# Operations on freshly loaded tiles are issued behind their engine's earlier work, and attention takes slightly less dense work beside it

## The chip, the cores and the metric

The kernel runs on one core of one Trainium2 chip. The metric is device time in microseconds (us): the median of three runs before the change is 2832.04 us, the runs lie between 2825.74 and 2834.8 us. TensorE (PE in the profile) multiplies matrices, VectorE (DVE) and ScalarE (ACT) work on tiles in SBUF and PSUM, GpSimd (POOL) does a few fills, and SyncE (SP) issues nearly all DMAs. Each engine works through its own list of instructions in the order in which the built program has them. An instruction that waits for a DMA or for another engine holds up everything behind it on its own list.

## The reference, cut to what matters

One encoder layer runs over two sequences, of 1024 and 2048 tokens (samples 0 and 1 below), with 16 learned tokens ahead of each.

```python
xn = _rmsnorm(h, g_pre)
proj = xn @ w_in + b_in
na_q, na_k, na_v, na_z, ml_qk, ml_v, ml_z, ml_o, ml_g, mg = jnp.split(proj, SPLIT_IDX, axis=-1)
ya = _neighbourhood_attention(na_q, na_k, na_v, na_rpb)
ya = (ya * jax.nn.silu(na_z)) @ w_a
yb = (_mlstm_branch(ml_qk, ml_v, ml_g, ml_o, ml_conv_w, ml_head_g) * jax.nn.silu(ml_z)) @ w_b
ga, gb = jnp.split(jax.nn.sigmoid(mg), 2, axis=-1)
y = (ga * ya + gb * yb) @ w_out
return h + _rmsnorm(y, g_post)
```

Attention has 8 heads of width 64 with a window of 8 rows and 16 columns; the mLSTM has 4 heads of width 128 and runs in chunks, forward and backward. All is float32: each product is made of three products of a high and a low part (hi times hi, hi times lo, lo times hi).

## The kernel before

Two programs are woven into one order of TensorE instructions. **Dense** work is a list of groups (`PLAN`): input projections of 1024 tokens each, then six **merges** (`final`, L1464 to L1589), one for each block of 512 tokens. A merge multiplies the branch outputs by `w_a` and `w_b` in 8 steps of two products each (half `br` 1, the mLSTM, then `br` 0, attention), gates and adds them on DVE (L1502 to L1506), and then runs an output stage of 16 turns through `w_out` (L1536 to L1538). ACT squares each result (L1566) and DVE scales it by `g_post` into the tile `yo` (L1567). The residual rows `xres` are added behind that (`final_out`, L1617), beside the next merge's products. **Sparse** work is, in this order, the mLSTM of sample 0 (`ml`), attention of sample 0 (`na`), the mLSTM of sample 1 and attention of sample 1. Each sparse step yields a number of microseconds, and `run` (L1669) draws dense work of that planned length behind it: `A_NA` for a step of attention (four steps for one unit, 128 units in sample 1), `A_A` for a step of the mLSTM's second part.

TensorE's order is the order in which the code is written and drawn (`manual_schedule` for PE alone). The order on DVE, ACT, POOL and SP is made by a scheduler when the program is built: it goes by its own estimate of when each instruction can start, that of a DMA's landing included. So an operation on a tile that a DMA fills can be placed well ahead of where the code has it.

What the change touches:

- `na_prep` (L804): for each attention head, `qr`, `kr` and `vr` are loaded and split into high and low parts (L835, L840, L845 on ACT, L838, L842, L847 on DVE).
- `conv` (L1060): the first tap of the mLSTM's convolution on the loaded tile `raw` (L1066, ACT).
- `ml_outputs` (L1215): `kv` splits the loaded `kf` (L1267), `decay` adds the triangular mask to the loaded `um` (L1274, DVE; then two exponentials on ACT, L1276), `state` splits the loaded `va` into `vh` (L1284, ACT) and `vl` (L1285, DVE). A block of 256 tokens takes six steps: scores of block b+1 (TensorE into the bank `sc`, which DVE reads at L1308), then `back(b, 0)`, whose products read `vh` and `vl`, and so on; `finish` and, for every second block, the head's norm (`ml_norm`, L1398 to L1422) follow.
- `yload` (L1425): a merge's eight tiles `yl` (four of attention, from `ya`; four of the mLSTM, from `yb`) are loaded at least seven calls ahead, copied to `yh` (L1455, ACT) and reduced to the low part (L1440, DVE). It runs beside the output stage of the merge before.
- `final` L1520: the one scaling of the loaded `g_post` row (`gain`), and `final_out` L1617.

Of the kernel before, what the change touches and what calls it, by code (L numbers as in the profile page):

```python
# [2 lines left out]

# [1 line left out]

# [4 lines left out]
F32 = mybir.dt.float32  # L10
F32R = mybir.dt.float32r
I32 = mybir.dt.int32
AF = mybir.ActivationFunctionType
ALU = mybir.AluOpType
# [100 lines left out]

NBW = 4
C512, C256 = 0.235, 0.12
A_NA, A_D, A_A, A_G = 1.1, 1.63, 1.82, 1.3


class K:
# [15 lines left out]
    def rsqrt8(self, pool, v, shape):  # L137

        nc = self.nc
        y = pool.tile(shape, F32, name="nwy", bufs=2)  # L140
        t = pool.tile(shape, F32, name="nwt", bufs=2)
        nc.vector.tensor_scalar(y.bitcast(I32), v.bitcast(I32), 1, None, op0=ALU.logical_shift_right)
        nc.vector.tensor_scalar(y.bitcast(I32), y.bitcast(I32), -1.0, MAGIC, op0=ALU.mult, op1=ALU.add)
        for n in range(3):
            nc.vector.scalar_tensor_tensor(t, y, 0.25 ** n, y, op0=ALU.mult, op1=ALU.mult)
            nc.vector.tensor_tensor(t, t, v, op=ALU.mult)
            nc.vector.scalar_tensor_tensor(y, t, 3.0, y, op0=ALU.subtract, op1=ALU.mult)
        return y

    def psum(self, tag, shape):  # L150
        return self.pp.tile(shape, F32, name=tag, tag=tag, bufs=BANKS[tag])
# [652 lines left out]
    def na_prep(self, np_, s, rows, heads, j):  # L804

        nc, i = self.nc, self.i
        rt, pr, hh = heads[j]
        typ, lo, nr = rows[rt]
        ns, h0 = nr + 1, hh * 64
        ms, rs = ((nr, 0), (nr, 0), (0, 1))[typ]  # L810
        qr = np_.tile([P, 512], F32, name="qr", bufs=1)
        stk = np_.tile([P, 4, P], F32R, name="stk", bufs=2)
        qb = self.qB[hh]
        nc.sync.dma_start(qr[0:64], self.NQ[s][pr][h0:h0 + 64, rt * 512:(rt + 1) * 512])
        sv = stk.rearrange("p b t -> p (b t)")
        kr = np_.tile([P, 16, 64], F32, name="kr", bufs=1)
        kd = np_.tile([P, 16, 64], F32R, name="kd", bufs=2)
        kx = self.kx[hh]
        self.twice(kr[:, rs:rs + nr, :].rearrange("p a b -> p (a b)"), self.NK[s][pr], h0, lo * 64)
        self.twice(kr[:, ms, :], self.NKM[pr], h0, 0)  # L820
        ks = 8 * ns
        if hh == 0:
            self.vr = np_.tile([P, 8, P], F32, name="vr", bufs=1)
            f0 = pr * P
            nc.sync.dma_start(self.vr[ms * 8:ms * 8 + 8], self.NVM[:, f0:f0 + P].rearrange("(b c) f -> c b f", c=8))
            nc.sync.dma_start(self.vr[rs * 8:(rs + nr) * 8],
                              self.NV[s][:, lo * 8:(lo + nr) * 8, f0:f0 + P].rearrange("b q f -> q b f"))
            self.zt = np_.tile([P, 512], F32, name="zt", bufs=2)
            nc.sync.dma_start(self.zt, self.NZ[s][pr][:, rt * 512:(rt + 1) * 512])
            self.yg = np_.tile([P, 512], F32, name="yg", bufs=2)  # L830
        vr, zt, yg = self.vr, self.zt, self.yg
        if j < 2 or rows[heads[j - 2][0]][0] != typ:
            nc.gpsimd.dma_start(kx[64:128, :ns, :].rearrange("p a b -> p (a b)"), i["masks"][typ, :, :ns * 64])
        yield
        nc.scalar.activation(sv[0:64], qr[0:64], AF.Copy)  # L835
        yield
        nc.scalar.activation(qb[0:64], stk[0:64].bitcast(F32), AF.Copy)
        nc.vector.tensor_tensor(sv[64:128], qr[0:64], sv[0:64].bitcast(F32), op=ALU.subtract)  # L838
        yield
        nc.scalar.activation(kd[:, :ns, :], kr[:, :ns, :], AF.Copy)  # L840
        yield
        nc.vector.tensor_tensor(kx[0:64, :ns, :], kr[0:64, :ns, :], kd[0:64, :ns, :].bitcast(F32), op=ALU.subtract)  # L842
        vt = np_.tile([P, 8, 2, 64], F32R, name="vt", bufs=2)
        vv = vr[:ks, :, h0:h0 + 64]
        nc.scalar.activation(vt[:ks, :, 0], vv, AF.Copy)  # L845
        yield
        nc.vector.tensor_tensor(vt[:ks, :, 1], vv, vt[:ks, :, 0].bitcast(F32), op=ALU.subtract)  # L847
        self.head = stk, qb, kd, vt, yg, zt
        yield
# [210 lines left out]
    def conv(self, mp, raw, h, is_k, n):  # L1060

        nc = self.nc
        w0 = (12 if is_k else 0) + 3 * h
        w = [self.cw[:, w0 + j:w0 + j + 1] for j in range(3)]
        c = mp.tile([P, BL], F32, name="cv", bufs=1)
        nc.scalar.activation(c[:, :n], raw[:, 0:n], AF.Copy, scale=w[0])  # L1066
        yield
        for j in (1, 2):
            nc.vector.scalar_tensor_tensor(c[:, :n], raw[:, j:j + n], w[j], c[:, :n], op0=ALU.mult, op1=ALU.add)
        th = mp.tile([P, BL], F32, name="th", bufs=1)  # L1070
        nc.scalar.activation(th[:, :n], c[:, :n], AF.Tanh, scale=0.5 / (S_K if is_k else 0.5))
        yield th, c
# [142 lines left out]
    def ml_outputs(self, mp, s, h, g, NB, sts, norms):  # L1215
# [46 lines left out]
        def kv(b):  # L1262
            if b < NB:
                kf = kfs.pop(b)
                kh = mp.tile([P, CB, P], F32R, name="kh", tag="kh", bufs=2)
                kl = mp.tile([P, CB, P], F32R, name="kl", tag="kl", bufs=2)
                nc.scalar.activation(f2(kh), kf, AF.Copy)  # L1267
                nc.vector.tensor_tensor(f2(kl), kf, f2(kh).bitcast(F32), op=ALU.subtract)
                kss[b] = kh, kl

        def decay(b, d):
            if b < NB:
                um = ums[b][d]
                nc.vector.tensor_tensor(um, um, self.trim[:, d], op=ALU.add)  # L1274
                for j in range(CB):
                    nc.scalar.activation(um[:, j], um[:, j], AF.Exp, bias=g[d]["a"][:, 1 + b * CB + j, h:h + 1])  # L1276

        def state(b):

            if b < NB:  # L1280
                va = vas.pop(b)
                vh = mp.tile([P, CB, 130], F32R, name="vh", bufs=1)
                vl = mp.tile([P, CB, 130], F32R, name="vl", bufs=1)
                nc.scalar.activation(f2(vh), f2(va), AF.Copy)  # L1284
                nc.vector.tensor_tensor(f2(vl), f2(va), f2(vh).bitcast(F32), op=ALU.subtract)  # L1285
                vs[b] = vh, vl
                for j in range(CB):
                    cc = b * CB + j
                    if cc:
                        prev = sts[(cc - 1) // CB][:, (cc - 1) % CB, 0:130]  # L1290
                        now = sts[b][:, j, 0:130]
                        nc.vector.scalar_tensor_tensor(now, prev, g[0]["f"][:, cc, h:h + 1], now, op0=ALU.mult, op1=ALU.add)
                cch = mp.tile([P, CB, 260], F32R, name="cch", bufs=1)
                ccl = mp.tile([P, CB, 260], F32R, name="ccl", bufs=1)
                nc.scalar.activation(f2(cch), f2(sts[b]), AF.Copy)
                nc.vector.tensor_tensor(f2(ccl), f2(sts[b]), f2(cch).bitcast(F32), op=ALU.subtract)
                cs[b] = cch, ccl
# [127 lines left out]
    def yload(self, s, b):  # L1425
# [11 lines left out]
            todo.append((k, step + 7))  # L1437

        def low(k):
            nc.vector.tensor_tensor(yl[:, k], yl[:, k].bitcast(F32), yh[:, k].bitcast(F32), op=ALU.subtract)  # L1440
            self.yk.add(k)

        late, half = [4, 5, 6, 7, 0, 1, 2, 3], None
        while todo or late or half is not None:
            for k in tuple(late):
                if (("ml", s) if k > 3 else ("na", s, b, k)) in self.done:
                    late.remove(k)
                    load(k)
            if half is not None:
                low(half)  # L1450
                half = None
            idle = True
            if todo and (step >= todo[0][1] or self.need):
                half = todo.popleft()[0]
                nc.scalar.activation(yh[:, half], yl[:, half].bitcast(F32), AF.Copy)  # L1455
                idle = False
            step += 1
            yield "wait" if idle else None
# [5 lines left out]
    def final(self, s, b, nxt):  # L1464
# [52 lines left out]
        hook = None  # L1517
        if self.fresh:
            self.fresh = False
            nc.vector.tensor_scalar(self.gpost, self.gpost, -0.125, None, op0=ALU.mult)  # L1520
        if not nxt:
            self.last = []
            for tt in range(4):
# [66 lines left out]
    def final_out(self, s, t0, yt, ssq, a, b):  # L1590
# [19 lines left out]
        for tt in range(a, b):  # L1610
# [3 lines left out]
            x = None if self.last else xr.popleft()  # L1614
            for c in (slice(0, 512), slice(512, D)):
                y = yt[tt][:, c]
                nc.vector.scalar_tensor_tensor(y, y, r[:, tt - a:tt - a + 1], self.last.pop(0) if self.last else x[:, c], op0=ALU.mult, op1=ALU.add)  # L1617
                nc.sync.dma_start(out[t0 + tt * P:t0 + tt * P + P, c], y)
                if c.start:
                    load(tt + 2)  # L1620
                yield
# [123 lines left out]
```

## Time and profile before

| what | value |
|---|---|
| median of three runs | 2832.04 us |
| the profiled execution's own time | 2829.43 us |
| its span, first to last instruction | 2827.7 us |
| mean granted TensorE clock | 0.997 |
| busy: PE, DVE, ACT | 2790.4, 1795.5, 1306.9 us |
| DMA engines' mean busy share (queue q1) | 69.9% |
| attention of sample 1 and the merges beside it | about 2058 to 2720 us of the span |

Shares of busy time are means over stages with different limits. In the timeline, a number in brackets is the time for which the engine was idle just before the instruction, with the instruction or DMA that ended it behind the arrow. A row of groups gives count, busy time, mean length of one, and the idle time ahead of them. Lines of DVE, ACT and PE carry line numbers of the kernel before.

### The profile page before, as it was taken

The numbers are of one execution on the slowest core, as the hardware profiler recorded it, in microseconds if no ns is written. First come the engines' busy times: TensorE is split into PE (matmuls) and PEld (weight loads), VectorE is DVE, ScalarE is ACT, GpSimd is POOL, SyncE is SP. The second block draws the span as 40 slices with busy tenths as digits, with TensorE's granted clock in tenths as the row PEclk, the third lists the DMA queues.
The fourth block names the chain that finished last, engine by engine and source line by source line (L and its number), as shares of the span: only waits on it lengthen the run. The fifth ranks groups of instructions, "written<-read, shape, count | busy, mean of one in ns | idle before, by whom it ended". The sixth has DMA issues, their size and how long they took to land.

```text
span 2827.7 us, 49161 instructions
## 1 busy us (share of the span) xinstructions
PE 2790.4 (99%) x17312; PEld 2482.6 (88%) x17312; DVE 1795.5 (63%) x4931; ACT 1306.9 (46%) x3135; POOL 16.2 (1%) x103
## 2 busy tenths in 40 slices
PE   9999999999999999999999999999999999999998
PEld 7998898999899988988988888888888988989888
DVE  5232687676466654456667666474679888787854
ACT  5122556444444444355456555463455554545421
POOL 0000000000000000000000000000000000000000
PEclk9999999999999999999999999999999999999999
DMA  9555768755975554676657785656679999898964
GB/s 367 184 187 185 265 200 308 256 183 171 342 236 156 177 157 147 188 272 188 203 177 229 254 276 189 190 175 195 188 217 366 295 306 300 257 297 256 314 247 167
DMA packets 378281, 655.13 MB, mean 232 GB/s; under 512 B 50897, under 2 KB 199841, under 8 KB 378033
## 3 DMA queue, kind: packets, MB, share of 16 engines
q1 hardware_dynamic: 376912, 649.29, 69.9%
q0 software_dynamic: 1120, 2.69, 0.4%
q8 instruction: 137, 2.24, 0.3%
q14 instruction: 112, 0.91, 0.1%
HBM read 449.61 MB, written 202.22 MB: 231 GB/s over the span
## 4 chain that ended last, share of the span: by engine, by line
PE 86%; DMA 5%; DVE 5%; ACT 1%; issue 1%; SPq 1%; DVEq 0%; ACTq 0%
PE pj L156 15%; PE pj L157 15%; PE pj L158 15%; PE pj L577 7%; PE pj L578 6%; PE pj L579 6%; PE sm L907 3%; PE pj L1536 3%; PE pj L1538 3%; PE pj L1537 3%; PE tr L892 2%; PE sm L158 1%; PE sm L157 1%; PE sm L156 1%; DMA yl<-yb 1%
## 5 line engine op out<-in xcount | busy, mean ns | idle before, releaser
L156 PE MATMUL pj<-xh,whi 128*128 128x512 f32 (+1 forms) x1792 | 705.2, 394 | 0.8 <-ACT whi L250 0.8
L157 PE MATMUL pj<-xl,whi 128*128 128x512 f32 (+1 forms) x1792 | 689.0, 384 | 0.4 <-DVE xl L322 0.4
L158 PE MATMUL pj<-xh,wlo 128*128 128x512 f32 (+1 forms) x1792 | 687.9, 384 | 0.3 <-DVE wlo L251 0.3
L577 PE MATMUL pj<-whi,xh 128*128 128x256 f32 (+3 forms) x1576 | 449.8, 285 | 1.5 <-ACT st L507 1.5
L578 PE MATMUL pj<-wlo,xh 128*128 128x256 f32 (+3 forms) x1576 | 444.0, 282 | 0.0
L579 PE MATMUL pj<-whi,xl 128*128 128x256 f32 (+3 forms) x1576 | 443.7, 282 | 0.0
L158 PEld LDWEIGHTS pj<-xh,wlo 128*128 128x128 f32 x1792 | 336.9, 188 | 71.9 <-DVE wlo L251 0.5
L156 PEld LDWEIGHTS pj<-xh,whi 128*128 128x128 f32 x1792 | 337.2, 188 | 61.2 <-ACT whi L250 1.6
L157 PEld LDWEIGHTS pj<-xl,whi 128*128 128x128 f32 x1792 | 337.5, 188 | 57.6 <-issue 1.0
L577 PEld LDWEIGHTS pj<-whi,xh 128*128 128x128 f32 (+1 forms) x1576 | 293.6, 186 | 3.2 <-ACT st L507 1.9
L579 PEld LDWEIGHTS pj<-whi,xl 128*128 128x128 f32 (+1 forms) x1576 | 293.3, 186 | 0.9
L578 PEld LDWEIGHTS pj<-wlo,xh 128*128 128x128 f32 (+1 forms) x1576 | 293.2, 186 | 1.0
L1536 PE MATMUL pj<-whi,mh 128*128 128x256 f32 x768 | 220.2, 287 | 2.3 <-DVE yo L1567 2.3
L1538 PE MATMUL pj<-whi,mlo 128*128 128x256 f32 x768 | 216.7, 282 | 0.0
L1537 PE MATMUL pj<-wlo,mh 128*128 128x256 f32 x768 | 216.7, 282 | 0.0
L899 DVE TENSOR_TENSOR pts<-tr,pts 96x512 fp32r<-96x512 f32 (+2 forms) x192 | 131.4, 684 | 81.3 <-ACT pts L894 80.3
L894 ACT ACTIVATE pts<-tr 96x512 fp32r<-96x512 f32 (+2 forms) x192 | 113.8, 593 | 121.2 <-PE tr L892 121.0
L156 PE MATMUL pj<-yh,whi 128*128 128x512 f32 x384 | 156.1, 407 | 6.2 <-ACT yh L1455 4.8
L158 PE MATMUL pj<-yh,wlo 128*128 128x512 f32 x384 | 152.7, 398 | 0.0
L157 PE MATMUL pj<-yl,whi 128*128 128x512 f32 x384 | 152.4, 397 | 0.0
L1536 PEld LDWEIGHTS pj<-whi,mh 128*128 128x128 f32 x768 | 145.5, 189 | 4.4 <-DVE yo L1567 2.5
L1537 PEld LDWEIGHTS pj<-wlo,mh 128*128 128x128 f32 x768 | 145.7, 190 | 1.8
(278 smaller groups left out, 5018.0 us busy)
## 6 DMA issues: line engine op xcount, KB each, us to landing
whi<-wh SPq DMA_DIRECT2D x176, 512.0 KB
wlo<-wl SPq DMA_DIRECT2D x176, 512.0 KB
wraw<-wu SPq DMA_DIRECT2D x64, 512.0 KB
wh<-whi SPq DMA_DIRECT2D x64, 512.0 KB
wl<-wlo SPq DMA_DIRECT2D x64, 512.0 KB
gt<-st SPq DMA_DIRECT2D x96, 256.0 KB
tg<-gt SPq DMA_DIRECT2D x96, 256.0 KB
xt<-xt SPq DMA_DIRECT2D x32, 512.0 KB
```

The lines of the kernel that those rows point to most:

```text
L156: mm(out, ah, bh, start=start, stop=False)
L157: mm(out, ah, bl, start=False, stop=False)
L158: mm(out, al, bh, start=False, stop=stop)
L577: nc.tensor.matmul(o, xh, wh, start=k == 0, stop=False)
L578: nc.tensor.matmul(o, xh, wl, start=False, stop=False)
L579: nc.tensor.matmul(o, xl, wh, start=False, stop=k == KT - 1)
L894: nc.scalar.activation(pts[:ks, :, 0, :], pt[:ks], AF.Copy)
L899: self.nc.vector.tensor_tensor(pts[:ks, :, 1, :], pt[:ks], pts[:ks, :, 0, :].bitcast(F32), op=ALU.subtract)
L907: nc.tensor.matmul(av[:, :256], vt[:ks, kc // 8 + ch].rearrange("p a b -> p (a b)"), pts[:ks, ch].rearrange("p a b -> p (a b)"), start=ch ...
L1536: nc.tensor.matmul(o, mh[:, k, xs], wh, start=k == 0, stop=False)
L1537: nc.tensor.matmul(o, mh[:, k, xs], wl, start=False, stop=False)
L1538: nc.tensor.matmul(o, ml[:, k, xs], wh, start=False, stop=k == KT - 1)
```

## The change

A new helper looks for the instructions written last for DVE and for ACT, and makes whatever is written inside its block stand behind them on those engines. No semaphore is added and no instruction is added or taken away; the number of each kind of instruction is the same on every engine. Twelve places are wrapped in it. `A_NA` goes from 1.1 to 1.085.

```diff
-A_NA, A_D, A_A, A_G = 1.1, 1.63, 1.82, 1.3
+A_NA, A_D, A_A, A_G = 1.085, 1.63, 1.82, 1.3
...
+    @contextmanager
+    def held(self):
+
+        with ExitStack() as st:
+            left = {mybir.EngineType.DVE, mybir.EngineType.Activation}
+            for x in reversed(self.nc.cur_bb.bb.instructions):
+                if x.engine in left:
+                    left.remove(x.engine)
+                    st.enter_context(self.tc.issue_after(x))
+                    if not left:
+                        break
+            yield
...
-        nc.scalar.activation(sv[0:64], qr[0:64], AF.Copy)
+        with self.held():
+            nc.scalar.activation(sv[0:64], qr[0:64], AF.Copy)
...
-        nc.scalar.activation(c[:, :n], raw[:, 0:n], AF.Copy, scale=w[0])
+        with self.held():
+            nc.scalar.activation(c[:, :n], raw[:, 0:n], AF.Copy, scale=w[0])
...
-                nc.vector.tensor_tensor(um, um, self.trim[:, d], op=ALU.add)
+                with self.held():
+                    nc.vector.tensor_tensor(um, um, self.trim[:, d], op=ALU.add)
...
-                nc.scalar.activation(f2(vh), f2(va), AF.Copy)
+                with self.held():
+                    nc.scalar.activation(f2(vh), f2(va), AF.Copy)
...
-            nc.vector.tensor_tensor(yl[:, k], yl[:, k].bitcast(F32), yh[:, k].bitcast(F32), op=ALU.subtract)
+            with self.held():
+                nc.vector.tensor_tensor(yl[:, k], yl[:, k].bitcast(F32), yh[:, k].bitcast(F32), op=ALU.subtract)
...
-            nc.vector.tensor_scalar(self.gpost, self.gpost, -0.125, None, op0=ALU.mult)
+            with self.held():
+                nc.vector.tensor_scalar(self.gpost, self.gpost, -0.125, None, op0=ALU.mult)
...
-                nc.vector.scalar_tensor_tensor(y, y, r[:, tt - a:tt - a + 1], self.last.pop(0) if self.last else x[:, c], op0=ALU.mult, op1=ALU.add)
+                with self.held():
+                    nc.vector.scalar_tensor_tensor(y, y, r[:, tt - a:tt - a + 1], self.last.pop(0) if self.last else x[:, c], op0=ALU.mult, op1=ALU.add)
```

The other wrapped places are the copies of `kr` and `vr` in `na_prep`, of `kf` in `kv`, and of `yl` to `yh` in `yload`.

Three places show what moves. The first is DVE behind the first merge, where the residual is added (L1617 before, L1641 after) between the next merge's evacuations (L1502, after L1524) and attention's work. Before:

```order
L146 TENSOR_TENSOR nwt<-nwt,sv 128x4
L147 SCALAR_TENSOR_TENSOR nwy<-nwt,nwy 128x4
L1617 SCALAR_TENSOR_TENSOR yo<-yo,nwy,xres 128x512 x4
L899 TENSOR_TENSOR pts<-tr,pts 128x4x128
L1502 SCALAR_TENSOR_TENSOR tg<-tg,pj 128x512
L922 TENSOR_TENSOR yg<-sm,yg 64x8x16
```

On DVE at the same place after the change:

```order
L852 TENSOR_TENSOR stk<-qr,stk 64x512
L1524 SCALAR_TENSOR_TENSOR tg<-tg,pj 128x512
L1641 SCALAR_TENSOR_TENSOR yo<-yo,nwy,xres 128x512
L1528 TENSOR_TENSOR mlo<-tg,mh 128x512
L1641 SCALAR_TENSOR_TENSOR yo<-yo,nwy,xres 128x512
L915 TENSOR_TENSOR pts<-tr,pts 128x4x128
L938 TENSOR_TENSOR yg<-sm,yg 64x8x16
```

Four additions that stood in a row are now taken one at a time, with evacuations between them, and later.

The second place is ACT in the output stage of the second merge, where `yl` is copied to `yh` (L1455 before, L1477 after) between the squares (L1566, after L1589) and attention's exponentials and copies. Before:

```order
L1566 ACTIVATE sqj,ssq<-pj 128x256
L1455 ACTIVATE yh<-yl 128x512
L875 ACTIVATE prb,sm<-sc,mx 128x512
L894 ACTIVATE pts<-tr 128x4x128
L1566 ACTIVATE sqj,ssq<-pj 128x256
L915 ACTIVATE yg<-sm 64x8x16
L1455 ACTIVATE yh<-yl 128x512 x3
L1566 ACTIVATE sqj,ssq<-pj 128x256
```

On ACT in an output stage after the change:

```order
L1589 ACTIVATE sqj,ssq<-pj 128x256
L1477 ACTIVATE yh<-yl 128x512
L891 ACTIVATE prb,sm<-sc,mx 128x512
L910 ACTIVATE pts<-tr 128x4x128
L855 ACTIVATE kd<-kr 128x1024
L1589 ACTIVATE sqj,ssq<-pj 128x256
L1477 ACTIVATE yh<-yl 128x512
L931 ACTIVATE yg<-sm 64x8x16
L891 ACTIVATE prb,sm<-sm,mx 128x512
L861 ACTIVATE vt<-vr 128x8x64
L1589 ACTIVATE sqj,ssq<-pj 128x256
L1477 ACTIVATE yh<-yl 128x512
```

The copies come one to a turn of the stage, in its later half, where three or more stood together in its first half.

The third place is DVE in the mLSTM of sample 0, second head, from the third block's `state` to the last block's scores: `vl` is L1285 before and L1305 after, the reading of the scores L1308 and L1328, the mask's addition L1274 and L1293, the low part of the next input tiles L460 and L473. Before:

```order
L1285 TENSOR_TENSOR vl<-va_3093,vh 128x260
L1069 SCALAR_TENSOR_TENSOR cv<-raw,cw,cv 128x256
L1343 RECIPROCAL den<-den 128x4
L1069 SCALAR_TENSOR_TENSOR cv<-raw,cw,cv 128x256
L452 SCALAR_TENSOR_TENSOR xt<-xt,gpre,rx 128x512 x5
L1351 SCALAR_TENSOR_TENSOR hb<-num,den,hb 128x128
L452 SCALAR_TENSOR_TENSOR xt<-xt,gpre,rx 128x512
L1351 SCALAR_TENSOR_TENSOR hb<-num,den,hb 128x128
L1144 SCALAR_TENSOR_TENSOR kf<-th,cv 128x256
L1308 TENSOR_TENSOR um<-um,sc 128x256 x2
```

On DVE at the same place after the change:

```order
L1328 TENSOR_TENSOR um<-um,sc 128x256
L1428 BN_AGGR mv<-bs 128x2
L473 TENSOR_TENSOR xl<-xt,xh 128x2x512
L1428 BN_AGGR mv<-bs 128x2 x2
L1293 TENSOR_TENSOR um<-um,trim 128x256
L473 TENSOR_TENSOR xl<-xt,xh 128x2x512 x3
L1335 TENSOR_TENSOR sl<-um,sh 128x256
L1430 TENSOR_SCALAR mv<-mv 128x4
L1328 TENSOR_TENSOR um<-um,sc 128x256
L1305 TENSOR_TENSOR vl<-va_3093,vh 128x260
```

`vl` stood ahead of the reading of the next scores and now stands behind it, with the mask's addition and four low parts between.

Besides, the scaling of `gain` stands on DVE behind 1 of the first merge's 16 gatings (L1502) before and behind 15 of them after. On PE, 25 instructions of an output stage stand between attention's last product (L907) and the last merge before, and 133 after. On POOL four or five small fills (of `raw` and `st`) move by a place or two. On SP, loads and stores change places with their neighbours: half of its 2254 rows move by at most 3 places, nine in ten by at most 10. The largest moves are loads of `raw` and `kf` in the mLSTM of sample 0 (up to 43 rows later), and the stores of `yo` with the loads of `xres`, which move with the additions that they belong to (up to 30 rows later).

More of the change, by code (lines that the diff above doesn't have):

```diff
@@ L1 @@
 from collections import deque
-from contextlib import ExitStack
+from contextlib import ExitStack, contextmanager
 import numpy as np
@@ L839, in na_prep @@
         yield
-        nc.scalar.activation(kd[:, :ns, :], kr[:, :ns, :], AF.Copy)
+        with self.held():
+            nc.scalar.activation(kd[:, :ns, :], kr[:, :ns, :], AF.Copy)
         yield
@@ L844, in na_prep @@
         vv = vr[:ks, :, h0:h0 + 64]
-        nc.scalar.activation(vt[:ks, :, 0], vv, AF.Copy)
+        with self.held():
+            nc.scalar.activation(vt[:ks, :, 0], vv, AF.Copy)
         yield
@@ L1439, in low @@
         def low(k):
-            nc.vector.tensor_tensor(yl[:, k], yl[:, k].bitcast(F32), yh[:, k].bitcast(F32), op=ALU.subtract)
+            with self.held():
+                nc.vector.tensor_tensor(yl[:, k], yl[:, k].bitcast(F32), yh[:, k].bitcast(F32), op=ALU.subtract)
             self.yk.add(k)
@@ L1454, in yload @@
                 half = todo.popleft()[0]
-                nc.scalar.activation(yh[:, half], yl[:, half].bitcast(F32), AF.Copy)
+                with self.held():
+                    nc.scalar.activation(yh[:, half], yl[:, half].bitcast(F32), AF.Copy)
                 idle = False
@@ L1519, in final @@
             self.fresh = False
-            nc.vector.tensor_scalar(self.gpost, self.gpost, -0.125, None, op0=ALU.mult)
+            with self.held():
+                nc.vector.tensor_scalar(self.gpost, self.gpost, -0.125, None, op0=ALU.mult)
         if not nxt:
@@ L1616, in final_out @@
                 y = yt[tt][:, c]
-                nc.vector.scalar_tensor_tensor(y, y, r[:, tt - a:tt - a + 1], self.last.pop(0) if self.last else x[:, c], op0=ALU.mult, op1=ALU.add)
+                with self.held():
+                    nc.vector.scalar_tensor_tensor(y, y, r[:, tt - a:tt - a + 1], self.last.pop(0) if self.last else x[:, c], op0=ALU.mult, op1=ALU.add)
                 nc.sync.dma_start(out[t0 + tt * P:t0 + tt * P + P, c], y)
```

2 lines of the change are left out of this document (1 added, 1 removed).

## The prediction

> **What bounds the kernel now.** I read the page first (span, busy shares, chain), then PE's waits, then busy time by stretch.
>
> ```profile
> span 2827.7 us, 49161 instructions
> PE 2790.4 (99%) x17312; PEld 2482.6 (88%) x17312; DVE 1795.5 (63%) x4931; ACT 1306.9 (46%) x3135; POOL 16.2 (1%) x103
> PE 86%; DMA 5%; DVE 5%; ACT 1%; issue 1%; SPq 1%; DVEq 0%; ACTq 0%
> 0.00:2058.00 2058.00, 2049.73 (x12573) 1815.88 (x12574) 1207.35 (x3538) 950.50 (x2276) 14.01 (x99) 1.00 0.65 215
> 2058.00:2736.00 678.00, 657.64 (x4198) 590.80 (x4197) 547.75 (x1288) 344.26 (x820) 2.19 (x4) 0.99 0.88 284
> 2736.00:2828.00 92.00, 83.06 (x544) 75.91 (x543) 40.42 (x107) 12.14 (x40) 0.00 (x0) 0.96 0.59 211
> ```
>
> A stretch's row has its length, then busy time (and count) of PE, PEld, DVE, ACT and POOL, the granted clock, the DMA engines' busy share and GB/s. The kernel is bound by TensorE. PE is idle for 2058.00 − 2049.73 = 8.3 us up to attention of sample 1, for 678.00 − 657.64 = 20.4 us beside that attention and its merges, and for 8.9 us in the last 92. No product is added or removed, so the change can win only idle time and time at a lowered clock, most of it between 2058 and 2736 us; and it can add waits in the first stretch, where there are almost none. Most of the idle time has these names (engine and line that waits, what it waits for: total us, count, longest):
>
> ```profile
> PE sm L861 <- DVE yg L922: 5.1, 5, 3.3
> PE pj L156 <- ACT yh L1455: 4.8, 1, 4.8
> PE sm L907 <- ACT prb L875: 2.8, 2, 2.0
> PE pj L1536 <- DVE yo L1567: 2.3, 1, 2.3
> ```
>
> **The change part by part.** The durations come from the profiled execution, 2829.43 us against a span of 2827.7; it lies 2.6 us below the median, 2832.04, and the sum is made against it.
>
> *Term A, `gain`.*
>
> ```profile
> 2125.22 0.69 DVE L1520 TENSOR_SCALAR gain<-gain 128x1024 f32<-128x1024 f32 x1 [4.04 <-DMA gain<-g_post]
> 2126.57 0.50 PE L156 MATMUL pj<-yh,whi 128*128 128x512 f32 x1 [1.34 <-DVE tg L1502]
> 2135.66 0.92 PE L907 MATMUL sm<-pts,vt 96*128 96x256 f32 x4 [2.02 <-ACT prb L875]
> 2136.06:2139.46 3.40, 3.40 (x11) 2.73 (x11) 3.37 (x7) 0.77 (x2) 0.00 (x0) 0.50 1.04 413
> ```
>
> DVE stood 4.04 us before the load of `gain`, with the first merge's gatings and attention's work queued behind it. PE lost 1.34 and 2.02 us, and half of the 3.40 us that followed at clock 0.50, 1.7 us: 5.1 us. With 15 gatings ahead of it instead of one, the scaling meets a landed tile. I take all of it.
>
> *Term B, the last merge's attention inputs.*
>
> ```profile
> 2717.45 0.64 PE L907 MATMUL sm<-pts,vt 104*128 104x256 f32 x4
> 2717.93 0.28 PE L1536 MATMUL pj<-whi,mh 128*128 128x256 f32 x1
> 2718.05 0.28 PE L1537 MATMUL pj<-wlo,mh 128*128 128x256 f32 x1
> 2729.92 0.63 ACT L1455 ACTIVATE yh<-yl 128x512 fp32r<-128x512 f32 x1 [8.38 <-DMA yl<-ya]
> 2730.60 0.79 PE L156 MATMUL pj<-yh,whi 128*128 128x512 f32 x1 [4.84 <-ACT yh L1455]
> 2729.98:2736.80 6.82, 6.20 (x14) 4.60 (x15) 4.24 (x7) 1.20 (x2) 0.00 (x0) 0.50 0.95 357
> ```
>
> From attention's last product at 2717.45 the chain goes through the store of `ya`, its load and the copy, to 2730.55: 13.1 us. Two products of the output stage start 0.12 us apart, so the 108 more of them that the order puts in between (133 against 25) are 108 × 0.12 = 13.0 us of further cover for a wait of 4.84 us. The copy's own load keeps its place ahead of the last stores on SP. Gain: 4.84 and half of the 6.20 busy us at clock 0.50, 3.1: 7.9 us. The dense work behind attention is what the smaller `A_NA` leaves over: 4 × 128 × 0.015 = 7.7 us by its plan. Attention's own chain loses that cover, 0.06 us in a unit; all its waits on `prb` above are 2.8 us, so I put this at nothing, with an end of some 2.8 us if they doubled.
>
> *Terms C and D, clumps and waits at the head of DVE and ACT beside attention.*
>
> ```profile
> 2240.57 2.74 DVE L1617 SCALAR_TENSOR_TENSOR yo<-yo,nwy,xres 128x512 f32<-128x512 f32 x4
> 2379.88 0.47 PE L861 MATMUL sm<-kd,stk 128*128 128x512 f32 x1 [3.26 <-DVE yg L922]
> 2380.00:2386.00 6.00, 6.00 (x31) 4.99 (x32) 5.71 (x13) 2.17 (x5) 0.00 (x0) 1.00 1.05 387
> 2507.00 1.42 DVE L1617 SCALAR_TENSOR_TENSOR yo<-yo,nwy,xres 128x512 f32<-128x512 f32 x2 [3.24 <-DMA xres<-x_sample]
> 2511.75 0.48 PE L861 MATMUL sm<-kd,stk 128*128 128x512 f32 x1 [1.04 <-ACT prb L875]
> 2312.64 0.71 PE L907 MATMUL sm<-pts,vt 128*128 128x256 f32 x4 [1.10 <-DVE yg L922]
> 2427.50 0.63 ACT L1455 ACTIVATE yh<-yl 128x512 fp32r<-128x512 f32 x1 [1.74 <-DMA yl<-yb]
> 2432.14 0.39 PE L1536 MATMUL pj<-whi,mh 128*128 128x256 f32 x1 [2.31 <-DVE yo L1567]
> 2433.02:2436.42 3.40, 3.40 (x16) 3.21 (x16) 3.39 (x8) 2.62 (x8) 0.00 (x0) 0.50 0.56 167
> 2678.43 0.74 PE L907 MATMUL sm<-pts,vt 104*128 104x256 f32 x4 [0.73 <-ACT prb L875]
> ```
>
> C, the residual additions: they come four in a row (2.74 us of DVE), or stand 3.24 us for `xres`; PE's waits behind them are 3.26 and 1.04 us, 4.3 together. D, the copies to `yh`: one stood 1.74 us for its load, and PE waited 2.31 with 3.40 us at half clock behind it (1.7); with 1.10 and 0.73 elsewhere this is 5.8 us. The change spreads the additions among the evacuations and puts the copies later, one to a turn. But no work goes: DVE is busy for 547.75 of 678.00 us here, 81%, so some waits will form anew. Ends: nothing, and all 10.1 us. In the order after, the first merge's eight copies still come within one unit of attention, so I take three quarters: 7.6 us.
>
> A, B, C and D: 5.1 + 7.9 + 7.6 = **20.6 us** gained.
>
> *The price: `vl` in the mLSTM.*
>
> ```profile
> 477.65 0.42 DVE L1285 TENSOR_TENSOR vl<-va,vh 128x260 fp32r<-128x260 f32 x1
> 481.94 0.28 PE L158 MATMUL sc<-qh,kl 128*128 128x128 f32 x1
> 483.91 0.28 PE L157 MATMUL sm<-vl,sh 128*128 128x130 f32 x1
> 1899.95 0.33 PE L157 MATMUL sm<-vl,sh 128*128 128x130 f32 x1 [0.51 <-DVE vl L1285]
> L1308 DVE TENSOR_TENSOR um<-um,sc 128x256 f32<-128x256 f32 x96 | 36.0, 414 | 34.9 <-PE sc L158 34.7
> L460 DVE TENSOR_TENSOR xl<-xt,xh 128x1024 fp32r<-128x1024 f32 x16 | 18.9, 1221 | 3.6 <-ACT xh L459 3.6
> L322 DVE SCALAR_TENSOR_TENSOR xl<-xt,gpre,xh 128x512 fp32r<-128x512 f32 x24 | 16.8, 748 | 7.3 <-ACT xh L321 7.3
> L1274 DVE TENSOR_TENSOR um<-um,trim 128x256 f32<-128x256 f32 x96 | 40.0, 423 | 101.1 <-DMA um<-ud 100.7
> L1410 DVE TENSOR_SCALAR mv<-mv 128x4 f32<-128x4 f32 x24 | 4.0, 166 | 0.3
> ```
>
> `vl` needs only its load and `vh`, so it stood ahead of the next scores' reading and was ready 483.91 − 478.07 = 5.8 us before its product. Held behind `decay`, which is held in turn behind the norm's part, it stands behind that reading in 23 of 40 transitions between blocks. PE wants it 483.91 − 481.94 = 2.0 us after the last product of the scores starts, 2.4 with the norm's transposes between, and some 3.4 to 3.9 where more dense work is drawn there. The reading twice and `vl` itself (0.83 + 0.42) fit into that. In five transitions they don't:
>
> - Head 2 of sample 0, the place shown: two readings 0.83, four low parts 4 × 1.22 = 4.88, the mask's addition and its like on `sl` 0.85, small statistics 0.6, `vl` 0.42: 7.6 us, 5.6 beyond 2.0.
> - Head 4 of sample 1, at the step to its last block: seven L322 at 0.75 = 5.2, with readings, small ones and `vl` 6.9; beyond 2.4: 4.5. Two blocks earlier, six of them with the mask's addition: 4.5 beyond 3.9.
> - Two more with the norm's or `finish`'s pieces between: 1.9 and 1.5.
>
> Together 18.0 us. The ends are 0 (if dense work drawn ahead of the product covers it all) and 18.0. Nearest to the durations above is the upper end; I take three quarters, 13.5, and as much of a half-clock stretch of 3.4 us (1.7 lost) behind each of the three waits over 4 us: 3 × 1.7 × 3/4 = 3.8. The old wait of 0.51 goes. **Loss: 16.8 us.** The other 17 of the 23 transitions have `vl` behind the readings with a few small operations; nine of them come within 0.35 us of the limit, and I put them at nothing, with 3.2 us as the end.
>
> The row ahead of the clock's share: 4.84 us of waiting brought 0.50 for 6.8 us, 2.31 us brought it for 3.4, and 3.26 us brought none (clock 1.00 behind it). The Trainium skill ("TensorE: Matmul & The Clock Gate", "Part 1: The HAM clock gate (the "warmup" mystery)") says that the clock is halved after an idle window of about 3.4 us, which runs free of the program, and released after a busy one. By that rule each of the three long waits costs a window for certain, so 5.1 us and not 3.8, and the sum would be 1.3 us higher; the halving after 2.31 us speaks against the rule as a threshold, the 6.8 us after 4.84 for its window.
>
> *What costs nothing.* The splits of `na_prep` still stand a unit of attention or more ahead of their products; that unit's dense and sparse products hide them, and if it failed, each head would pay about a split, under 1 us. `conv`, `kf` and the loads that SP issues later with them belong to a block's preparation, a block ahead of its scores; POOL's fills are 2.19 us in all from 2058. SP waits for no addition that was not ahead of its store before.
>
> **The sum.** 2829.4 − 20.6 + 16.8 = 2825.6: **2826 us**. Its own range, with C and D at both ends and the price between 8 and 25, is 2818 to 2835.
>
> **The rivals.**
>
> *`vl` comes in time* (faster). The scores' reading on DVE is itself idle for 34.9 us in all, waiting for PE; where DVE runs ahead, the five lists shrink, and PE draws dense work between. For it: 18 of the 23 transitions fit anyway. Against it: L460 and L322 stand behind a reading that can't start before the scores end. It gives 2829.4 − 20.6 − 0.5 = 2808, called 2809.
>
> *`vl` waits in full, at half clock* (slower than before). The place is the same five transitions, 18.0 us; the three waits over 4 us each behave as the 4.84 did (3.1 lost, not 1.7), 9.3 us, and the nine close ones pay 0.35 each, 3.2: 30.5. It gives 2829.4 − 20.6 + 30.5 = 2839. It decides against the change from a loss above 20.6 us, and visibly from about 29.
>
> *The merges' waits form anew.* Spreading doesn't help on a DVE that is 81% busy: A and B stay, C and D give nothing: 2829.4 − 13.0 + 16.8 = 2833.
>
> *The order doesn't matter* because the waits are for DMAs, whatever is issued when: the mean DMA share in this stretch is 0.88. Against it: B needs no faster DMA, only more cover. It lies inside the third rival.
>
> **How the numbers follow.** A measurement of this kernel can tell about 0.3%, 8.5 us, from no change: faster is below some 2823 of the median, slower above 2840. Chances: forecast 0.46 (of which 0.07 fall below, 0.37 within, 0.02 above), `vl` in time 0.31 (0.30 faster), new waits in the merges 0.10, `vl` in full 0.13 (0.12 slower). Faster 0.37, same 0.49, slower 0.14. The range goes from 2806, under the first rival, to 2840, over the second.
>
> **What would show it.** A: DVE's wait ahead of the scaling gone, and no half clock at about 2136. B: no wait over 1 us of PE on `yh` at the last merge. C and D: PE's waits on `yg` L922 and `yo` L1567 down to a quarter. The price: waits of PE on `vl` that sum to about 14 us, the longest in head 2 of sample 0 at about 484 us, with half clock behind it; PE's idle time up to 2058 us grows from 8.3 to some 22. If these waits are under 3 us, the price was wrong and the time is near 2809; if new waits stand between 2058 and 2736 at other lines, C and D were.

## The result, and the profile after

The changed kernel takes 2849.91 us (median of 6 runs, 2845.15 to 2854.95) against 2832.41 before: a ratio of 1.0064, with a 95% interval of 1.0048 to 1.0079. It is slower by 17.5 us, above the range that was predicted. The profiled execution took 2845.15 us.

The page of the changed kernel, its span, busy time and chain:

```profile
span 2843.3 us, 48991 instructions
...
PE 2793.5 (98%) x17312; PEld 2485.9 (87%) x17312; DVE 1800.3 (63%) x4931; ACT 1301.4 (46%) x3135; POOL 15.8 (1%) x103
...
PE 92%; DMA 3%; DVE 3%; ACT 1%; issue 1%; SPq 0%; DVEq 0%; ACTq 0%
```

Busy time by stretch in the changed kernel. The cuts, 2093 and 2752 us, are put where TensorE has issued as many products as at 2058 and 2736 before (12573 and 4201 against 12573 and 4198):

```profile
0.00:2093.00 2093.00, 2059.87 (x12573) 1823.44 (x12574) 1214.56 (x3545) 950.87 (x2280) 13.76 (x99) 0.99 0.64 211
2093.00:2752.00 659.00, 651.38 (x4201) 587.27 (x4200) 541.57 (x1275) 338.44 (x816) 2.04 (x4) 1.00 0.89 290
```

So the two halves of the forecast can be read apart. The first stretch, with the mLSTM, is 2093 − 2058 = **35 us longer**: TensorE's idle time there went from 8.3 to 2093.00 − 2059.87 = 33.1 us, and its busy time, for the same products, rose by 10.1 us. The second, attention of sample 1 and its merges, is 678 − 659 = **19 us shorter**: idle time 20.4 to 7.6, and 6.3 us less busy. What follows is 0.4 us shorter: 35 − 19 − 0.4 = 15.6, the difference of the spans.

What TensorE waits for in the changed kernel (engine and line that waits, what it waits for: total us, count, longest):

```profile
PE sm L169 <- ACT vh L1304: 12.6, 5, 4.8
PE sc L169 <- ACT qh L1275: 7.8, 1, 7.8
PE sm L170 <- DVE vl L1305: 5.9, 6, 3.0
PE sm L923 <- ACT prb L891: 3.9, 3, 1.6
PE sm L877 <- DVE yg L938: 2.0, 1, 2.0
```

The waits on `yh`, on `yo` and most of those on `yg` have gone. In their place stand `vh` and `vl`, 18.5 us together, and one wait of 7.8 us on `qh`, which the forecast had not seen.

The timeline of the changed kernel at the place that the prediction showed, head 2 of sample 0 (start, duration, engine and line, operation; in brackets the idle time before and what ended it). L465 and L473 are dense work, the scaling and low part of the next input tiles; L1293 is the mask's addition, L1295 the exponentials behind it:

```profile
491.14 0.28 PE L171 MATMUL sc<-qh,kl 128*128 128x128 f32 x1
...
491.45 3.39 DVE L465 SCALAR_TENSOR_TENSOR xt<-xt,gpre,rx 128x512 f32<-128x512 f32 x5
...
494.85 0.39 DVE L1328 TENSOR_TENSOR um<-um,sc 128x256 f32<-128x256 f32 x1
...
496.51 0.39 DVE L1293 TENSOR_TENSOR um<-um,trim 128x256 f32<-128x256 f32 x1
...
496.82 3.49 DVE L473 TENSOR_TENSOR xl<-xt,xh 128x1024 fp32r<-128x1024 f32 x3
...
496.93 0.69 ACT L1295 ACTIVATE um<-um,g_a 128x128 f32<-128x128 f32 x2 [0.70 <-DVE um L1293]
...
497.53 0.40 ACT L1304 ACTIVATE vh<-va 128x260 fp32r<-128x260 f32 x1
...
497.99 0.45 PE L169 MATMUL sm<-vh,sh 128*128 128x130 f32 x1 [4.77 <-ACT vh L1304]
...
500.63 0.41 DVE L1328 TENSOR_TENSOR um<-um,sc 128x256 f32<-128x256 f32 x1
...
500.96 0.42 DVE L1305 TENSOR_TENSOR vl<-va,vh 128x260 fp32r<-128x260 f32 x1
...
501.44 0.47 PE L170 MATMUL sm<-vl,sh 128*128 128x130 f32 x1 [2.99 <-DVE vl L1305]
...
497.99:504.50 6.51, 3.52 (x11) 2.94 (x12) 6.05 (x22) 0.42 (x1) 0.00 (x0) 0.50 1.00 333
```

`vh` itself is late. ACT does not stand waiting for its tile: the copy stands behind the exponentials of the next block, these wait for the mask's addition, and the addition stands on DVE behind dense pieces and the norm. TensorE waits 4.77 us for `vh`, then 2.99 for `vl` behind three low parts and the second reading, and runs at clock 0.50 up to 504.5 at least.

In sample 1's fourth head the same two tiles are late for another reason. There the exponentials don't wait for DVE; they and `vh` stand on ACT behind eight dense scalings, 5.01 us (L334, timeline of the changed kernel):

```profile
1886.44 5.01 ACT L334 ACTIVATE xh<-xt,gpre 128x512 fp32r<-128x512 f32 x8
...
1892.73 0.69 ACT L1295 ACTIVATE um<-um,g_a 128x128 f32<-128x128 f32 x2
1893.31 0.42 ACT L1304 ACTIVATE vh<-va 128x260 fp32r<-128x260 f32 x1
...
1893.78 0.33 PE L169 MATMUL sm<-vh,sh 128*128 128x130 f32 x1 [2.50 <-ACT vh L1304]
```

### The profile page after: what moved, and what is told of

The parts are those of the page before. It is cut to its first block, busy times and chain, and to the rows that moved or that the text cites. A ratio compares the mean times of both kernels' runs of the same rounds, so it can differ in the third digit from the quotient of the medians.

```text
span 2843.3 us, 48991 instructions
## 1 busy us (share of the span) xinstructions
PE 2793.5 (98%) x17312; PEld 2485.9 (87%) x17312; DVE 1800.3 (63%) x4931; ACT 1301.4 (46%) x3135; POOL 15.8 (1%) x103
## 4 chain that ended last, share of the span: by engine, by line
PE 92%; DMA 3%; DVE 3%; ACT 1%; issue 1%; SPq 0%; DVEq 0%; ACTq 0%
PE pj L169 16%; PE pj L170 16%; PE pj L171 16%; PE pj L590 6%; PE pj L591 6%; PE pj L592 6%; PE pj L1559 3%; PE pj L1561 3%; PE pj L1560 3%; PE sm L923 3%; PE tr L908 3%; PE sm L170 1%; PE sm L171 1%; PE sm L169 1%; PE sc L877 1%
```

## The experiments

The changed kernel has eleven holds (not twelve, as said ahead of the diff): three in attention's preparation (`qr`, `kr`, `vr`), four in the mLSTM (`raw`, `kf`, `um`, `va`) and four for the merges (`yl` to `yh`, its low part, `gain`, the residual additions). All ratios are against the kernel before, measured beside; its median was between 2828.97 and 2832.41 us in the four sets of runs, so kernels of different sets are compared by their ratios. "First" and "second" are the lengths of the two stretches in the profiled execution, cut at the same TensorE instruction (within 5).

| kernel | median us | ratio, 95% interval | first | second |
|---|---|---|---|---|
| before | 2832.41 | 1 | 2058 | 678 |
| changed | 2849.91 | 1.0064, 1.0048 to 1.0079 | 2093 | 659 |
| e1, mLSTM's holds out | 2814.1 | 0.9941, 0.9927 to 0.9956 | 2058 | 660 |
| e2, `raw` free | 2848.52 | 1.0062, 1.0048 to 1.0075 | 2094 | 662 |
| e3, `um` free | 2838.59 | 1.0029, 1.0017 to 1.0041 | 2080 | 664 |
| e4, `va` free | 2820.93 | 0.9967, 0.9954 to 0.998 | 2066 | 660 |
| e5, `A_NA` alone | 2828.91 | 0.9998, 0.9989 to 1.0008 | 2058 | 676 |
| e6, merges' holds alone | 2821.46 | 0.9973, 0.9962 to 0.9985 | 2059 | 671 |
| e8, `gain` alone | 2832.74 | 1.001, 0.9998 to 1.0022 | 2060 | 681 |
| e10, `raw` and `va` free | 2806.8 | 0.9918, 0.9901 to 0.9936 | 2051 | 665 |
| e7, mLSTM's holds alone | 2854.68 | 1.0092, 1.0076 to 1.0109 | 2082 | 684 |
| e11, `va` held alone | 2853.5 | 1.0086, 1.0071 to 1.0101 | 2085 | 680 |
| e12, e10 without preparation's holds | 2808.69 | 0.9929, 0.9916 to 0.9942 | 2052 | 664 |
| e13, `state` written first | 2829.07 | 1.0002, 0.9991 to 1.0013 | 2071 | 664 |

### Which hold makes the loss: e1 to e4

Each takes holds out of the changed kernel. e1 takes out all four of the mLSTM's:

```diff
-        with self.held():
-            nc.scalar.activation(c[:, :n], raw[:, 0:n], AF.Copy, scale=w[0])
+        nc.scalar.activation(c[:, :n], raw[:, 0:n], AF.Copy, scale=w[0])
...
-                with self.held():
-                    nc.scalar.activation(f2(kh), kf, AF.Copy)
+                nc.scalar.activation(f2(kh), kf, AF.Copy)
...
-                with self.held():
-                    nc.vector.tensor_tensor(um, um, self.trim[:, d], op=ALU.add)
+                nc.vector.tensor_tensor(um, um, self.trim[:, d], op=ALU.add)
...
-                with self.held():
-                    nc.scalar.activation(f2(vh), f2(va), AF.Copy)
+                nc.scalar.activation(f2(vh), f2(va), AF.Copy)
```

> The changed kernel with the holds on raw, kf, um and va (all of the mLSTM's) taken out; those on attention's preparation, the merges' inputs, gain and the residual additions stay, and so does A_NA 1.085. Theory 1 (the loss is made by the mLSTM's holds alone, the gain by the rest): about 2811 us, 0.993 of the kernel before; TensorE's idle time ahead of sample 1's attention falls from 33 us back to about 8, and no wait over 1 us on vh, vl or qh is left. Rival (the loss comes from elsewhere: SP's loads in another order, attention's preparation, the smaller cover): some of the waits stay and the time is above 2825.

e2 takes out the first of these edits' holds only, on `raw`:

> The changed kernel with only the hold on the convolution's first tap on raw taken out. Theory 1: the wait of 7.77 us on qh in sample 0's second head goes, with the half clock behind it, and the waits on vh and vl (18.5 us together) stay: about 2840 us, 1.003. Rival (qh is late for its load, which SP issues later): the 7.77 us stay and the time is that of the changed kernel, 2850.

e3 the third only, on `um`:

> The changed kernel with only the hold on the mask's addition to um taken out. Theory 1a (vh is held behind the exponentials, and these wait for the held addition: the two holds make the loss together, and either release mends it): the 18.5 us on vh and vl fall below 5, the 7.77 us on qh stay, about 2828 us, 0.9985. Rival 1b (the hold on va alone is enough, since vh stands behind all that was written last whatever um does): the waits stay, 2850 us, 1.006.

e4 the fourth only, on `va`:

> The changed kernel with only the hold on vh's copy of va taken out. Theories 1a and 1b both: the 18.5 us on vh and vl go, the 7.77 us on qh stay: about 2827 us, 0.998. Rival 1c (the held additions and exponentials alone block ACT and DVE ahead of vh): more than half of the waits stay, above 2838 us.

e1 came out as expected, 2814.1 us, with the first stretch back at 2058: the whole loss is made by the mLSTM's holds, and the gain by the rest. So did e4's waits: those on `vh` and `vl` are gone and the one on `qh` stays, alone at the head of TensorE's waits; the time, 2820.9, is 6 us below the 2827 expected:

```profile
PE sc L169 <- ACT qh L1275: 7.8, 1, 7.8
PE sm L923 <- ACT prb L891: 3.3, 2, 2.6
```

e3 lies between its two theories: 5.1 us on `vh` and 1.5 on `vl` are left of 18.5, and waits of 5.1 us stand on `kf`, `kl` and `kh`, where the changed kernel has 1.2; 2838.6 where 1a gave 2828 and 1b 2850. Both count: without the held addition the wait in head 2 of sample 0 goes, and the 5.1 us left, in head 4 of sample 0, come where the copy of `vh` stands behind `finish`. e2 missed: `raw`'s wait went as foreseen, but the time stayed, because more came on `vh` (TensorE's waits of e2):

```profile
PE sm L169 <- ACT vh L1303: 20.9, 12, 5.8
PE sm L170 <- DVE vl L1304: 5.6, 13, 1.2
```

26.5 us where the changed kernel has 18.5 on `vh` and `vl` and 7.8 on `qh`. The rival, a late load, falls with the wait on `qh`. Releasing one hold made the other dearer: the prices don't add.

Why `qh` is late, in the timelines of the kernel before and then of the changed one:

```profile
424.44 0.42 ACT L1258 ACTIVATE qh<-cv 128x256 fp32r<-128x256 f32 x1
```

```profile
439.20 0.51 ACT L1083 ACTIVATE cv<-raw,cw 128x256 f32<-128x256 f32 x1
...
448.38 0.42 DVE L1272 SCALAR_TENSOR_TENSOR cv<-th,cv 128x256 f32<-128x256 f32 x1
...
448.83 0.42 ACT L1275 ACTIVATE qh<-cv 128x256 fp32r<-128x256 f32 x1 [2.99 <-DVE cv L1272]
...
449.30 0.48 PE L169 MATMUL sc<-qh,kh 128*128 128x128 f32 x1 [7.77 <-ACT qh L1275]
```

The first block of a head has no block ahead of it that would hide its convolution. Before, the scheduler ran it while the states of that head were still being summed, and `qh` stood ready at 424.86, over 17 us ahead of its first product at 442.32. Held, the first tap on `raw` starts at 439.20, and 9.6 us of steps on ACT and DVE, with other work between, lie between it and `qh`. Of the eight heads only this one waits for `qh`; why the others don't stays open.

### What makes the gain: e5, e6, e8, and e10

e5 is the kernel before with one number changed; e6 and e8 have `A_NA` 1.1, and only the merges' holds (L1460, L1477, L1543, L1641), or only that of `gain`:

```diff
-A_NA, A_D, A_A, A_G = 1.1, 1.63, 1.82, 1.3
+A_NA, A_D, A_A, A_G = 1.085, 1.63, 1.82, 1.3
```

> The kernel before with A_NA 1.085 alone, no holds. Theory (term B): 132 products of the output stage instead of 24 stand between attention's last product and the last merge, so TensorE's wait of 4.84 us on yh and the half clock behind it go: 7.9 us less, about 2824 us, 0.997. Waits A, C and D stay near 1.3 + 2.0, 3.3 and 2.3 us. Rival (the cover is given back, attention's own chains lose what the end wins): waits on prb and yg grow by 5 us or more, no change.

> The kernel before with the holds of the merges alone (yl to yh and its low part, gain, residual additions), A_NA 1.1, nothing held in the mLSTM or in attention's preparation. Theory: terms A, C and D, 5.1 + 7.6 = 12.7 us less, about 2819 us, 0.9955; the wait of 4.84 us at the last merge stays. Rival (DVE, 81% busy there, makes the waits anew): only A, 5.1 us, about 2827.

```diff
-            nc.vector.tensor_scalar(self.gpost, self.gpost, -0.125, None, op0=ALU.mult)
+            with self.held():
+                nc.vector.tensor_scalar(self.gpost, self.gpost, -0.125, None, op0=ALU.mult)
```

> The kernel before with only the scaling of gain held: 11 of the 16 gatings stand ahead of it instead of 1. Theory (term A): DVE's wait of 4.04 us and TensorE's 1.34 and 2.02 us with the half clock behind go, 5.1 us less, about 2827 us, 0.998; all else as before. Rival (the wait moves to another operation beside the first merge): waits of 3 us stay between 2090 and 2145 us, no change.

e5's rival has the time, no change, but not the waits: those on `prb` and `yg` stay where they were (4.1 and 6.1 us in all; 3.8 and 6.2 before). The wait at the last merge did go, but beside an earlier merge ACT stood at the head of its list for another load, and attention behind it (timeline of e5, then its second stretch):

```profile
2434.43 0.63 ACT L1468 ACTIVATE yh<-yl 128x512 fp32r<-128x512 f32 x1 [5.41 <-DMA yl<-yb]
...
2438.00 1.19 PE L920 MATMUL sm<-pts,vt 128*128 128x256 f32 x4 [3.95 <-ACT yh L1468]
...
2058.00:2734.00 676.00, 656.60 (x4205) 590.29 (x4203) 541.61 (x1278) 340.03 (x814) 2.04 (x4) 0.99 0.87 283
```

The kernel before has the same stand of ACT, 1.74 us long; with other cover it takes 5.41. e8 shows the same of term A (timeline of e8):

```profile
2127.78 0.69 DVE L1515 SCALAR_TENSOR_TENSOR tg<-tg,pj 128x512 f32<-128x512 f32 x1 [3.72 <-DMA tg<-gt]
...
2137.30 0.98 PE L920 MATMUL sm<-pts,vt 96*128 96x256 f32 x3 [3.47 <-DVE yg L935]
```

With `gain` out of the way DVE stands 3.72 us, at the same place, for the gating's own tile, and TensorE waits 3.47 us: the wait for a DMA was passed on to the next DMA. e6 won 7.5 us, between its theory (12.7) and its rival (5); the last merge's wait stays, 3.9 us, and a new one stands on a weight's load (timeline of e6):

```profile
2331.54 0.58 PE L1552 MATMUL pj<-whi,mh 128*128 128x256 f32 x1 [4.21 <-DMA whi<-wh]
```

So the holds and the smaller `A_NA` win 7 and 2 us of the second stretch alone, and 18 to 19 together (e1, and the changed kernel). Each leaves waits that the two together don't have: e6 its 3.9 us at the last merge, e5 its 3.95 and 1.50 us beside the earlier one. What became of the 4.21 us for the weight stays open.

e10 takes the holds on `raw` and `va` out of the changed kernel, the first and fourth edits of e1's diff:

> The changed kernel with the holds on raw and on va both taken out; those on kf and um stay. Theory (these two holds are the whole loss): no wait over 1.5 us on qh, vh or vl, time as with all four of the mLSTM's holds out, 2814 us, 0.994, or a few us less, since the release of va alone left only the 7.77 us on qh and brought 2821. Rival (as with raw alone, a release moves other waits into the mLSTM): new waits on vh or kf of 4 us and more, 2820 or above.

It beats both kernels, 2806.8 us, 0.9918; no wait on `qh`, `vh` or `vl` is among its largest, as its theory had it, and the time is 7 us below the 2814 expected. Against e1 it keeps the holds on `kf` and `um`: its first stretch is 7 us shorter and its second 5 longer, and the intervals overlap, so what these two do wasn't settled. By the ratios the release of `raw` is worth 14 us here (against e4), of which 7.8 are the wait, and the release of `va` 41 (against e2). Its largest wait is now a weight's load (TensorE's waits of e10):

```profile
PE pj L1557 <- DMA whi<-wh: 4.6, 1, 4.6
PE sm L923 <- ACT prb L891: 3.6, 3, 1.6
```

### What stands ahead of the hold: e7, e11, e12, e13

e7 and e11 add to the kernel before, with `A_NA` 1.1, the mLSTM's four holds, or only this:

```diff
-                nc.scalar.activation(f2(vh), f2(va), AF.Copy)
+                with self.held():
+                    nc.scalar.activation(f2(vh), f2(va), AF.Copy)
```

> The kernel before with the mLSTM's four holds alone (raw, kf, um, va), A_NA 1.1. Theory (the loss is theirs and adds up with the rest): the waits of 7.8 us on qh and some 18.5 us on vh and vl are there, and the time is the kernel before's plus what taking them out of the changed kernel won, 2849.9 - 2814.1 = 36: about 2865 us, 1.0127. Rival (the loss needs the other holds or the smaller cover as well): below 2850.

> The kernel before with the hold on vh's copy of va alone. Theory (the hold is dear where the held mask additions and their exponentials stand ahead of it): waits on vh and vl of 5 to 9 us together, no wait on qh, about 2838 us, 1.003. Rival (this hold alone makes the whole of the 18.5 us, or more, as when raw was released): 2850 us or above, 1.007.

e12 is e10 without the holds on `qr`, `kr` and `vr`:

> The changed kernel with the holds on raw and va and the three of attention's preparation (qr, kr, vr) out; the merges' holds, kf, um and A_NA 1.085 stay. Theory (these splits stand a unit or more ahead of their use, their holds neither win nor cost): the time of the kernel with raw and va free, 2807 us, within 4. Rival (the merges' holds win only with these, which keep ACT clear of loads that have not landed): 2812 us or above, with new waits of PE on yg or prb between 2050 and 2720 us.

e13 is the changed kernel with two lines exchanged:

```diff
-            decay(b + 1, 1)
-            state(b)
+            state(b)
+            decay(b + 1, 1)
```

> The changed kernel with all its holds, but state(b) written ahead of decay(b+1, 1) in the same step, so that vh's copy is held behind finish and no longer behind the second mask addition's exponentials. Theory (what stands last in the code ahead of the hold sets the price): the waits on vh and vl fall from 18.5 to below 9 us, the 7.8 us on qh stay, about 2835 us, 1.002. Rival (finish and the first mask addition hold vh up as much): 15 us and more stay, 2846 us or above.

e11's rival was right about the time: this hold alone costs 24.5 us, nearly as much as all four alone (e7, 25.7). The theory that the held additions make it dear falls. Its waits on `vh` and `vl` are 14.1 us, fewer than the rival's 18.5, and none is on `qh`; but TensorE's busy time in the first stretch rose by 11.2 us, to 2060.95, at the lowered clock behind these waits. Timeline of e11, where `um` is free and its exponentials were done by 1559.9:

```profile
1565.84 0.68 ACT L1364 ACTIVATE hb<-num,den 128x128 f32<-128x128 f32 x2
1566.43 0.40 ACT L1298 ACTIVATE vh<-va 128x260 fp32r<-128x260 f32 x1
...
1566.88 0.48 PE L169 MATMUL sm<-vh,sh 128*128 128x130 f32 x1 [2.90 <-ACT vh L1298]
```

Here it is `finish` of the block before, written earlier, behind which the copy of `vh` stands, and with it TensorE. The hold names only the instruction written last for ACT, the second exponential, and that was done 6.5 us earlier; why the built order has the copy behind `finish` as well isn't shown.

e13 changes what stands ahead of the hold. With `state` written ahead of the second `decay`, the copy is still held, and behind `finish` it is in time (timeline of e13):

```profile
486.66 0.68 ACT L1370 ACTIVATE hb<-num,den 128x128 f32<-128x128 f32 x2
...
488.07 0.41 ACT L1304 ACTIVATE vh<-va 128x260 fp32r<-128x260 f32 x1
...
492.59 0.22 PE L169 MATMUL sm<-vh,sh 128*128 128x130 f32 x1
```

`vh` is ready 4 us early. 0.9 us of waiting on `vh` are left in e13, and 1.2 on `vl`; with the 7.5 on `qh` the time is 2829.1, where 2835 was expected. So of the 35 us that the first stretch lost, two exchanged lines take back 22 (2093 to 2071); the second is 5 longer, and by the ratios the kernel gains 17 us. e7 stayed 10 us below its expectation, and above its rival's 2850: the first stretch grew by 24 us alone, and by 35 with the other holds and the smaller `A_NA` (2058 in e1, 2093). Its waits on `vh` and `vl` are 11.0 us instead of 18.5. Those of sample 0 are the changed kernel's, and those of sample 1 are nearly missing: the longest is 0.77 us, where the changed kernel has 3.87 twice. Why these need the other holds or the smaller `A_NA`, and why `va` alone waits behind `finish` when e13 doesn't, was not settled. e12 agrees with its theory: the preparation's holds neither win nor cost (2808.69 against 2806.8, the intervals overlap).

## Why the prediction was wrong

**The sign was wrong, by the size of the loss; the gain was nearly right in sum, in part by luck.** 20.6 us were forecast for the merges, 19 came, though A and B won nothing by themselves (e8, e5). 16.8 us were forecast for the mLSTM, 35 came: 24.8 of TensorE's idle time and 10.1 of its busy time. The sum's own range was also too narrow: the ends that it names give 2814 to 2841, not 2818 to 2835, which is still below what was measured.

- **The price of `vl`: the step of the sum that failed.** It was put at 16.8 us: three quarters of 18.0 us of waiting, and 3.8 us at half clock. The rival "in full" was nearest, and 10 us short itself (2839). Five transitions wait for more than 0.5 us: 7.76 us in head 2 of sample 0 (4.77 and 2.99), 1.66 in its head 4, 0.72, 3.87 and 3.87 in sample 1, 17.9 us in all. The three that were named by place are among them, at 7.76, 3.87 and 3.87 for 5.6, 4.5 and 4.5. So there was no cover for a quarter of it. The half clock was short too: TensorE's busy time rose by 10.1 us, where the forecast had 3.8 and the rival 9.3. It came in four places, and behind waits of 2.50 and 2.92 us as well.
- **The operation was only half right.** The forecast had `vl` late on DVE. Two thirds of the wait, 12.6 of 18.5 us, are for `vh`, on ACT. In head 2 of sample 0 it stands behind exponentials that wait for DVE, in head 4 of sample 1 behind 5 us of dense scalings on ACT itself. The sum took `vh` as there and had nothing of ACT's list. That the waits still come to the 18.0 us of DVE's durations is in part luck: for head 2 the list of 7.6 us also left out five scalings on DVE (L465, 3.39 us) between the scores and their first reading.
- **"What costs nothing" failed for `conv`.** It was put a block ahead of its scores; for a head's first block nothing stands ahead. That is 7.77 us of waiting, with 4.1 us at half clock behind it, in one head of eight. The rival's 30.5 us and these 7.8 + 2.1 make 40.4, more than the 35 of the stretch; the nine close transitions, 3.2 us in that sum, hardly came.
- **Term A (`gain`) was wrong though the wait went.** e8 shows 3.72 us for `tg` in place of 4.04 for `gain`, and no gain in time. In the changed kernel DVE stands 2.05 us for `tg`, and TensorE still waits 2.04 and 1.56 us beside that merge, for 1.34 and 2.02 before; only the half clock is gone. What the last rival said, that the load is late whatever is issued when, held here.
- **Term B was right in its place and not by itself.** No wait is left at the last merge, in the changed kernel and in e5. But e5 won nothing, since waits of 3.95 and 1.50 us on `yh` and `yo` came earlier: "I put this at nothing", said of attention's lost cover, is the line that failed there. Beside the holds the term has about its size: by the ratios e1 is 9 us faster than e6, which lacks the smaller `A_NA` and the preparation's holds, and those cost nothing (e12); 7.9 us were forecast.
- **Terms C and D** brought 7.5 us together with A in e6, for 12.7 in the forecast.
- **`na_prep`, POOL and SP cost nothing**, as said: e12 for the first, and e1, where the first stretch is as long as before, for the others.

## What to carry to other kernels

A scheduler that hoists an operation onto a freshly loaded tile can be right where the next product needs it, as here for `vh` and `raw`: pin an operation only if what is written ahead of it on its engine is done before its reader starts. Place and hold are one decision: two exchanged lines were worth 17 us here, as much as the merges' holds and `A_NA` together (e1). When a wait for a load is removed at the head of an engine's list, look for the next load in that list; it may land no earlier.

## What the runs showed of the hardware

In the changed kernel clock 0.50 came behind four waits of TensorE: 7.77 us (4.1 us of work at 0.50 behind it, and the same in e4, where that wait stays), 4.77 (with 2.99 inside the slow time, as shown above), and in sample 1 2.50 and 2.92, with 1.37 and 0.95 soon behind. A wait of 1.66 us, in head 4 of sample 0, left it at 1.00, and so did one of 2.04 beside the first merge. The stretches behind the 7.77, the 1.66, the 2.50 and the 2.92:

```profile
449.30:453.40 4.10, 4.10 (x12) 3.44 (x13) 1.08 (x3) 0.11 (x1) 0.00 (x0) 0.50 0.89 317
...
720.00:724.00 4.00, 3.77 (x18) 2.84 (x18) 3.60 (x14) 0.87 (x2) 0.00 (x0) 1.00 0.00 0
...
1895.00:1900.00 5.00, 4.52 (x13) 3.85 (x14) 4.79 (x22) 1.72 (x4) 0.00 (x0) 0.50 1.08 349
...
1930.00:1935.00 5.00, 5.00 (x14) 4.01 (x14) 3.22 (x13) 0.00 (x0) 0.00 (x0) 0.50 0.03 8
```

In e11 a wait of only 1.22 us for `vh`, with 0.39 for `vl` behind it, was followed by 0.51 from 1378.3 to 1381.8 us. So waits between 1.2 and 3.3 us may bring the half clock or not: length alone doesn't decide. In the clock records of these traces every slow stretch ahead of the kernel's end lasts 3.41 us or two or three times that, and begins a whole multiple of 3.41 us after the one before it, so where a wait falls on this grid may count as well. How much of such a span must be idle was not measured.

The Trainium skill ("TensorE: Matmul & The Clock Gate", "Part 1: The HAM clock gate (the "warmup" mystery)") puts the clock at half after an idle window of about 3.4 us. The waits of 7.77 and 4.77 us agree; those of 2.50 and 2.92 us here, and of 2.02 and 2.31 us in the kernel before, which were followed by 0.50 too, do not.
